# Attention gate's columns computed as seven products of halves, and attention groups merged where the last group is computed

## The chip, the cores and the metric

The kernel runs on one core of a Trainium2 chip. A core has five engines with a queue each: TensorE (PE in the profile; PEld is its weight load), VectorE (DVE), ScalarE (ACT), GpSimd (POOL) and SyncE (SP, which here only issues DMAs). An engine takes its instructions in the order in which they stand in its queue, and waits on semaphores of the others. The time is the device time of one execution in microseconds (us).

## The reference, cut to what matters

One decoder block on x of 2048 tokens x 1024 channels, in float32:

```python
h = rms_norm(x, norm_w) * (1 + scale) + shift
a, b, g_conv, q, k, v, g_attn, m_conv, m_attn = split(h @ w_in)   # 10240 columns
u = silu(layer_norm(conv31(a * sigmoid(b)))) * silu(g_conv);  y_conv = u @ w_conv_out
for g, (window, dilation) in enumerate(((128, 1), (512, 4), (2048, 16))):   # 4 heads of 128 each
    o[g], lse[g] = dilated_window_attention(q, k, v of the group's heads)
o = sum_g softmax_g(lse)[g] * o[g]            # the merge of the three groups, per token and head
y_attn = (o * silu(g_attn)) @ w_attn_out      # g_attn: 512 columns, the attention gate
x + gate * ((sigmoid(m_conv) * y_conv + sigmoid(m_attn) * y_attn) @ w_out)
```

## The kernel before, in words

Every float32 product is made of three TensorE products of halves of the mantissa (high x high, low x high, high x low), so each operand is kept as a `hi` and a `lo` tile. `h` lies transposed in SBUF in eight tiles for each of hi and lo: `(kh, t)` holds channels 512·kh on and tokens 512·t on.

The program has four stages that matter here.

1. **Units.** Twelve units, one for each group and head (`GROUPS = (1, 2, 0)`: the strided groups first, the dense one, group 0, last), each of 16 steps of 128 tokens. A step's `project_step` (L379) makes q, k, v of its tokens by `z_tokens` (L361, its matmul is L370): 24 matmuls of 128x384 into the bank `pz`, of which there are two. ScalarE then squares (L387), GpSimd takes the inverse root (L113, L114), VectorE normalises `qk` straight out of the bank (L398) and turns it (L405 to L408). After L398 the bank is free. The attention of a block of 128 queries is four parts (`attend_step`, L420): transposes `ptq`, scores `ps` with the row minimum and the exponential, transposes `ptp`, value product `po`. A `Flow` lays one part of each block in flight into the middle of a step's 24 matmuls; the order on TensorE is written by hand in this way, and the order on the other engines is set by a scheduler. Each block's output, with its row minimum and row sum (`osb`, 130 columns), goes to `acc_d` in DRAM for all three groups.
2. **Gate and merge.** 32 steps `(half, j)`, each of two heads and 128 tokens. `merge_z` (L497) is `z_tokens` with 256 of the gate's 512 columns into `pzg`. `merge_load` reads the three groups' outputs back from `acc_d`, `merge_weights` (L481) makes the groups' weights for two steps at a time, `merge_step` (L502) merges (L508, L510), takes the gate's silu by tanh (L513, L514), multiplies on GpSimd (L515) and transposes the product (`pta`, L520) into `ai_d`. The quarters S1 to S4, sums of quarters of `h` that were made earlier and lie in `s_d`, are split into hi and lo during the last of these steps, in place of tiles of `h` that are no longer needed.
3. **Conv and gates** (L885 on). Two halves of 1024 tokens, 20 jobs (`quad`, L940) in each: a job makes 2 x 128 columns for 1024 tokens as a 2x2 block product by seven products of 12 matmuls of 128x512 (with the sums S1 to S4 on the side of `h` and T1 to T4 on that of the weights), where eight would be needed directly. `column_steps` loads, combines and splits the weights. `ab_quad` makes the conv's input, `gate_quad` the other gates. The 31 taps of the conv run on VectorE, three or four operations per product (`run_conv`), beside the products.
4. **Projections** of the attention and conv branches, norm, output.

## Time and profile before

| | us |
|---|---|
| median of three runs | 2416.08 (2413.98 to 2416.86) |
| the profiled execution | 2415.89, its span 2414.0 |
| first gate matmul to first matmul of conv and gates | 1091.9 to 1205.1 |
| conv and gates | 1205.1 to 1966 |

TensorE is busy 98% of the span. In a timeline a row has start, duration, engine, line, operation and tiles, and in brackets the idle time before it with what ended it; matmuls overlap in their pipeline, so what one costs is the distance to the next start, not its duration. In windows the first number is the length, then come busy times with counts by engine and the granted TensorE clock (1.00 is full).

### The profile page before, as it was taken

How to read it: one execution, taken by the hardware profiler on the slowest of the kernel's cores; microseconds unless marked ns; L12 is line 12 of the kernel's file. 1: busy time of each engine (PE TensorE's matmuls, PEld its weight loads, DVE VectorE, ACT ScalarE, POOL GpSimd, SP SyncE). 2: the span in 40 equal slices, each digit the busy share in tenths (PEclk: the TensorE clock that was granted, in tenths of full speed). 3: DMA queues.
4: the chain of work that ended last, by engine and by line, in shares of the span. 5: the costliest groups of instructions: out<-in, count | busy, mean ns of one | idle time of the engine just before them, and what ended most of it. 6: DMA issues, size and time to landing. Idle time of an engine off the chain costs nothing.

```text
span 2414.0 us, 39453 instructions
## 1 busy us (share of the span) xinstructions
PE 2374.5 (98%) x12785; PEld 2119.2 (88%) x12785; DVE 1727.6 (72%) x3959; ACT 995.1 (41%) x2790; POOL 809.4 (34%) x931
## 2 busy tenths in 40 slices
PE   6999999999999999999999999999999999999999
PEld 2989999999999999999888888878888888878887
DVE  5855655555555565566879999989999977787654
ACT  5833433433444343444553444454444444332221
POOL 4421111111111111112357777775565530000221
PEclk8999999999999999999999999999999999999999
DMA  7633543544452222115654453674454469876553
GB/s 257 219 114 109 160 125 100 152 141 144 150 153 86 67 76 60 33 51 164 207 194 151 161 166 127 191 249 127 141 151 128 146 196 316 301 234 190 183 162 100
DMA packets 349467, 372.98 MB, mean 155 GB/s; under 512 B 29704, under 2 KB 251176, under 8 KB 349262
## 3 DMA queue, kind: packets, MB, share of 16 engines
q1 hardware_dynamic: 335966, 346.80, 46.3%
q10 hardware_dynamic: 13296, 23.66, 2.7%
q8 instruction: 102, 1.67, 0.3%
q14 instruction: 103, 0.84, 0.1%
HBM read 231.74 MB, written 138.61 MB: 153 GB/s over the span
## 4 chain that ended last, share of the span: by engine, by line
PE 90%; DMA 5%; DVE 2%; ACT 2%; POOL 1%; issue 1%; SPq 0%; ACTq 0%; DVEq 0%; POOLq 0%
PE pz L370 31%; PE paab L955 7%; PE yc L1231 6%; PE oa L1513 4%; PE ya L1231 4%; PE pag_g_d L955 4%; PE pag_mc_d L955 4%; PE pcab L955 3%; PE pag_ma_d L955 3%; PE pzg L370 3%; PE ps L442 3%; PE po L461 3%; PE oc L1513 2%; PE pcg_mc_d L955 2%; PE pcg_g_d L955 2%; PE ptq L432 2%
## 5 line engine op out<-in xcount | busy, mean ns | idle before, releaser
L370 PE MATMUL pz<-wh_u,hT_lo 128*128 128x384 f32 x1536 | 538.3, 351 | 5.8 <-DVE hT_lo L289 4.1
L370 PE MATMUL pz<-wh_u,hT_hi 128*128 128x384 f32 x1536 | 519.1, 338 | 4.6 <-ACT wh_u L346 2.6
L370 PE MATMUL pz<-wl_u,hT_hi 128*128 128x384 f32 x1536 | 520.1, 339 | 0.2
L398 DVE SCALAR_TENSOR_TENSOR qk<-pz,st,wqk 128x128 f32<-128x128 f32 x384 | 116.9, 346 | 319.9 <-POOL st L114 319.7
L113 POOL TENSOR_SCALAR st<-st 128x2 f32<-128x2 f32 x192 | 47.3, 246 | 814.5 <-ACT sq L387 814.5
L370 PEld LDWEIGHTS pz<-wh_u,hT_lo 128*128 128x128 f32 x1536 | 290.2, 189 | 9.0 <-DVE hT_lo L289 5.0
L370 PEld LDWEIGHTS pz<-wh_u,hT_hi 128*128 128x128 f32 x1536 | 291.4, 190 | 7.3 <-ACT wh_u L346 3.4
L370 PEld LDWEIGHTS pz<-wl_u,hT_hi 128*128 128x128 f32 x1536 | 290.5, 189 | 1.7 <-DVE wl_u L349 1.3
L434 ACT ACTIVATE qkT<-ptq 128x256 f32<-128x256 f32 x192 | 73.9, 385 | 419.9 <-PE ptq L432 419.4
L1033 DVE SCALAR_TENSOR_TENSOR ce<-us,pair_taps,ce 128x512 f32<-128x512 f32 x240 | 179.5, 748 | 1.7
L1004 DVE SCALAR_TENSOR_TENSOR ce<-ut,chan,ce 128x512 f32<-128x512 f32 x240 | 179.2, 747 | 0.0
L1017 DVE SCALAR_TENSOR_TENSOR cq<-ut,chan,cq 128x512 f32<-128x512 f32 x208 | 156.4, 752 | 4.2
L919 POOL TENSOR_TENSOR slT<-wT,shT 128x512 fp32r<-128x512 f32 x97 | 129.0, 1332 | 75.5 <-ACT shT L918 75.4
L387 ACT ACTIVATE sq<-pz 128x128 bf16<-128x128 f32 x384 | 106.2, 277 | 101.3 <-PE pz L370 94.4
L114 POOL TENSOR_TENSOR st<-st,mhalf 128x2 f32<-128x2 f32 x192 | 136.7, 712 | 16.0
L918 ACT ACTIVATE shB<-wB 128x512 fp32r<-128x512 f32 x120 | 75.5, 631 | 152.5 <-issue 44.5
L918 ACT ACTIVATE shT<-wT 128x512 fp32r<-128x512 f32 x100 | 63.1, 631 | 154.2 <-issue 65.7
L919 POOL TENSOR_TENSOR slB<-wB,shB 128x512 fp32r<-128x512 f32 x77 | 102.2, 1328 | 69.2 <-ACT shB L918 68.8
L447 ACT ACTIVATE sm<-sm,osb 128x128 f32<-128x128 f32 (+1 forms) x192 | 88.8, 462 | 62.1 <-DVE osb L445 59.1
L461 PE MATMUL po<-lv,pT 128*128 128x128 f32 x600 | 97.2, 273 | 0.0
L461 PEld LDWEIGHTS po<-lv,pT 128*128 128x128 f32 x600 | 93.0, 189 | 0.5 <-issue 0.5
L445 DVE CUSTOM_DVE_ANT_0 sm<-ps,mask 128x128 f32<-128x128 f32 (+1 forms) x192 | 68.2, 356 | 26.5 <-PE ps L442 26.4
(665 smaller groups left out, 6285.0 us busy)
## 6 DMA issues: line engine op xcount, KB each, us to landing
wB<-in_w_in_dram SPq DMA_DIRECT2D x140, 256.0 KB, 3.4
qkv_d<-qkv SPq DMA_DIRECT2D x128, 192.0 KB, 2.2
wT<-tT_d SPq DMA_DIRECT2D x80, 256.0 KB, 2.8
raw_u<-in_w_in_dram SPq DMA_DIRECT2D x93, 192.0 KB, 3.0
lqk<-qkv_d SPq DMA_DIRECT2D x128, 128.0 KB, 2.4
tT_d<-wB ACTq DMA_DIRECT2D x60, 256.0 KB, 2.8
acc_d<-osb SPq DMA_DIRECT2D x192, 65.0 KB, 1.7
at<-acc_d SPq DMA_DIRECT2D x64, 195.0 KB, 3.6
```

The source lines that it names most:

```text
L114: nc.gpsimd.tensor_tensor(dst, scratch[:, :n], mhalf[:, :n], op=ALU.pow)
L370: nc.tensor.matmul(pz[:, :width], part(a, k, P * j, P), w[:, :width], start=(m == 0), stop=(m == 23))
L398: nc.vector.scalar_tensor_tensor(qk[:, 2 * i : 2 * i + 2].rearrange("p a b -> p (a b)"), pz[:, P * i : P * i + P], st[:, 2 + i : 3 + i], w ...
L461: nc.tensor.matmul(po[:, :P], box["pT"][:, P * i : P * i + P], vt, start=(i == 0), stop=(i == nk - 1))
L918: nc.scalar.activation(h, q[name], AF.Copy)
L919: eng.tensor_tensor(l, q[name], h.bitcast(F32), op=ALU.subtract)
L955: nc.tensor.matmul(ps, w, x, start=(m == 0 and ps.name not in first), stop=(m == 11 and not more), skip_group_check=True)
L1004: stt(box["e"], e[:, 1 + j : 513 + j], chan[:, cb, 2 * j : 2 * j + 1], box["e"], op0=ALU.mult, op1=ALU.add)
L1017: stt(box["o"], o[:, 2 + j : 514 + j], w, psum_o, op0=ALU.mult, op1=ALU.add)
L1033: stt(dst, box["both"][:, 1 + j : 513 + j], pair_taps[:, cb, j : j + 1], box["e"], op0=ALU.mult, op1=ALU.subtract if j == 0 else ALU.add)
L1231: nc.tensor.matmul(pz, w, xx, start=(m == 0), stop=(m == len(terms) - 1))
L1513: nc.tensor.matmul(ps, y, w, start=(m == 0 and ps.name not in begun), stop=(m == 11 and not more), skip_group_check=True)
```

## The change

The gate's 512 columns leave stage 2, which is gone. They become four more jobs of stage 3, `ag_quad`, two in each half (jobs 15 and 17 of the first 22, and 38 and 39 of 44): seven products of 12 matmuls each. The job's `sink` takes silu of the product, loads the merged attention output `ai_d`, multiplies on GpSimd and writes `ag_d`, which the attention projection reads in place of `ai_d`.

The merge moves into the units of group 0 (the last four). Only groups 1 and 2 write to `acc_d`. A block of group 0 loads their 2 x 130 columns with its first part (`fetch`, issued on ScalarE's queue), and with its third part `weigh` makes the three weights for its 128 rows: a copy on GpSimd, five small operations on VectorE, one exponential and one scaled copy on ScalarE, and one 128x128 multiply-add on VectorE. `values` then multiplies and adds straight out of the bank `po`, where a copy stood. `turn_o`, a fifth part, transposes two blocks' outputs and stores them to `ai_d`.

The last unit goes through its blocks from 3 on, round to 2, so that the tiles of `h` come free in turn; S1, S2 and S3 are split in its steps 6 to 8 and 10 to 15, S4 among the first products. The attention of its last blocks, 7 turns, is laid between the first 13 products of stage 3, which begins with two gate jobs (one before). The strided blocks that run beside group 0 come every 2.5 steps (3.5 before), the sums for S1 to S4 in units 3 to 7 (4 to 10 before). The conv's operations are handed out at 2.9 and 3.1 per product.

```diff
+        def weigh():
+            st, part = box["st"], box["part"]
+            nc.gpsimd.tensor_copy(st[:, 0:2, 1:NG], part[:, :, P:].rearrange("p g k -> p k g"))
+            nc.vector.tensor_reduce(st[:, 4, 0:1], st[:, 0, :], op=ALU.min, axis=AX.X)
+            nc.scalar.activation(st[:, 2], st[:, 0], AF.Exp, scale=-1.0, bias=st[:, 4, 0:1])
+            nc.vector.tensor_mul(st[:, 3], st[:, 2], st[:, 1])
+            nc.vector.tensor_reduce(st[:, 4, 1:2], st[:, 3], op=ALU.add, axis=AX.X)
+            nc.vector.reciprocal(st[:, 4, 2:3], st[:, 4, 1:2])
+            nc.vector.scalar_tensor_tensor(st[:, 3], st[:, 2], 4.0, st[:, 4, 2:3].to_broadcast([P, NG]), op0=ALU.mult, op1=ALU.mult)
+            nc.scalar.activation(part[:, 0, :P], part[:, 0, :P], AF.Copy, scale=st[:, 3, 1:2])
+            nc.vector.scalar_tensor_tensor(part[:, 0, :P], part[:, 1, :P], st[:, 3, 2:3], part[:, 0, :P], op0=ALU.mult, op1=ALU.add)
...
+        def turn_o():
+            if j % 2 == 0:
+                return
+            pt = bank("t" if u == NG * NH - 1 and j in (13, 15, 1, 3) else "o", f"pta{n}")
+            for b, o in enumerate((state["even"], box["o"])):
+                nc.tensor.transpose(pt[:, P * b : P * b + P], o[:, :P], ident)
+            asb = mp.tile([P, 256], F32, tag="asb", name=f"asb{n}")
+            nc.scalar.activation(asb, pt[:, :256], AF.Copy)
+            nc.sync.dma_start(ai_d[h, :, P * j - P : P * j + P], asb)
...
+            if g == 0:
+                nc.vector.scalar_tensor_tensor(o[:, :P], po[:, :P], box["st"][:, 3, 0:1], box["part"][:, 0, :P], op0=ALU.mult, op1=ALU.add)
...
+        def fetch():
+            part = box["part"] = mp.tile([P, 2, ACC_W], F32, tag="part", name=f"part{n}", bufs=5)
+            nc.scalar.dma_start(part, acc_d[h][P * j : P * j + P])
...
-        pz = merge_z(0, j, cur, hooks)
...
-        turns += merge_step(half, j, pz, state)
...
+    def ag_quad(half, _, cb, got):
+        def sink(t, col, z, free=None):
+            th = z if free is None else free
+            sl = slice(1024 * half + 512 * t, 1024 * half + 512 * t + 512)
+            ait = gpa.tile([P, 512], F32, tag="ai", name=f"ag{half}_{cb}_{t}_{col}", bufs=2)
+            nc.sync.dma_start(ait, ai_d[cb + col, :, sl])
+            nc.scalar.activation(th, z, AF.Silu)
+            nc.gpsimd.tensor_mul(th, th, ait)
+            nc.sync.dma_start(ag_d[cb + col, :, sl], th)
...
+        todo[9 : 9] = [(ag_quad, half, None, cb) for cb in (0, 2)]
+        jobs += [todo.pop(0) for _ in range(2 - 2 * half)]
...
+        if at < TAIL and at % 2 == 0:
+            if own:
+                main.enter(own.pop(0))
+            for f in main.turn():
+                f()
```

VectorE, in the middle of a unit of group 0 (the last one, step 8, before; the third, step 8, after). `ps` are scores, `stm` the small tile of minima, sums and weights, `part` the other groups' outputs. Before:

```order
L445 ISA sm_5_13641,osb_5_13640<-ps_5_13637,mask 128x256
L445 ISA osb_5_13640 128x1
L349 TENSOR_TENSOR wl_ga_4_13654<-raw_ga_4_13651,wh_ga_4_13653 128x256
L462 COPY osb_14_13540<-po_14_13688 128x128
L398 SCALAR_TENSOR_TENSOR qk_8_13674<-pz_8_13608,st_8_13666,wqk 128x128 x2
L405 TENSOR_TENSOR t_8_13677<-qk_8_13674,tab_111 128x256
```

and after:

```order
L461 ISA sm_5_13071,stm_5_13070<-ps_5_13066,mask 128x256
L461 ISA stm_5_13070 128x1
L477 TENSOR_REDUCE stm_5_13070<-stm_5_13070 128x1
L350 TENSOR_TENSOR wl_u_4_13086<-raw_u_4_13083,wh_u_4_13085 128x384
L479 TENSOR_TENSOR stm_5_13070<-stm_5_13070 128x3
L480 TENSOR_REDUCE stm_5_13070<-stm_5_13070 128x1
L481 RECIPROCAL stm_5_13070<-stm_5_13070 128x1
L482 SCALAR_TENSOR_TENSOR stm_5_13070<-stm_5_13070 128x3
L461 ISA sm_14_13123,osb_14_13122<-ps_14_13120,mask 128x128
L461 ISA osb_14_13122 128x1
L484 SCALAR_TENSOR_TENSOR part_5_12983<-part_5_12983,stm_5_13070 128x128
L402 SCALAR_TENSOR_TENSOR qk_8_13106<-pz_8_13024,st_8_13098,wqk 128x128 x2
```

The whole of `weigh` now stands between a block's scores and the next normalisation out of `pz` (L398 before, L402 after).

TensorE, where stage 3 begins. Before, only transposes of the gated output stand among its first products; and ahead of it the gate matmuls, `pzg`, with a `pta` between them; a piece of them:

```order
L370 MATMUL pzg_3_15897<-wh_ga_0_14464,hT_hi_251 128x256
L370 MATMUL pzg_3_15897<-wl_ga_0_14465,hT_hi_251 128x256
L370 MATMUL pzg_3_15897<-wh_ga_0_14464,hT_lo_259 128x256
L520 MATMUL pta_1_15901<-ident,sg_1_15831 128x128 x2
L370 MATMUL pzg_3_15897<-wh_ga_1_14516,hT_hi_251 128x256
```

After, between the first product (`pag`) and the second (`pbg`) of stage 3:

```order
L897 MATMUL pag_g_d_0_15099<-hT_hi_252,first_w 128x512
L491 MATMUL pta_13_15124<-ident,osb_12_14725 128x128
L491 MATMUL pta_13_15124<-ident,osb_13_14812 128x128
L500 MATMUL po_14_15130<-lv_13_14568,pT_14_14974 128x128
L500 MATMUL po_14_15130<-lv_14_14659,pT_14_14974 128x128
L468 MATMUL ptp_15_15134<-ident,sm_15_14990 128x128 x2
L451 MATMUL ps_0_15148<-qkT_0_14998 128x128
L436 MATMUL ptq_1_15155<-ident,lqk_1_14931 128x128 x2
L897 MATMUL pbg_g_d_0_15100<-hT_hi_256,first_w 128x512
```

A whole turn of attention parts now lies there, and six more between the later ones.

ScalarE among the same products, before (one function table is loaded for the silu, and stays):

```order
L918 ACTIVATE shB_0_0_16025<-wB_0_0_15990 128x512
L918 ACTIVATE shB_0_0_16070<-wB_0_0_15992 128x512
L1081 ACT_TABLE_LOAD
L1081 ACTIVATE spare_hi<-spare_hi 128x512
L961 ACTIVATE spare_hi<-pag_g_d_0_16009 128x512
```

and after, in the seventh product:

```order
L860 ACTIVATE shB_0_2304_15347<-wB_0_2304_15086 128x512
L903 ACTIVATE spare_hi<-pag_g_d_0_15099 128x512
L493 ACTIVATE asb_15_15284<-pta_15_15281 128x256
L463 ACTIVATE sm_2_15309,stm_2_15308<-sm_2_15309,stm_2_15308 128x256
L1023 ACT_TABLE_LOAD
L1023 ACTIVATE spare_hi<-spare_hi 128x512
L463 ACT_TABLE_LOAD
L463 ACTIVATE sm_3_15319,stm_3_15316<-sm_3_15319,stm_3_15316 128x256
```

The silu of the gate job (L1023) and the exponential of the attention (L463) alternate here: five table loads stand where one stood, four more in all.

More of the change, by code (lines that the diff above doesn't have):

```diff
@@ L749, in tile_hybrid_block @@
                         extra.setdefault((14, 14, 23, 23)[i], []).append(lambda rest=rest: rest.pop(0)())
[L750 removed]
+                if u and 4 <= j < 4 + KC and not last_unit:
                     extra = spread_load(loads[j - 4])
[L752 removed]
+                for m, f in side.pop((u, p), ()):
                     extra.setdefault(m, []).append(f)
@@ L786, in tile_hybrid_block @@
-    turns = []
-    for j in range(3):
-        hooks = {}
-        for m in (4, 15):
-            if own and (j, m) != (0, 15):
-                main.enter(own.pop(0))
-            hooks[m] = main.turn()
-        pz = merge_z(0, j, cur, hooks)
-        if j < 2:
-            turns += merge_step(0, j, pz, state, "qkv", ("qk", "t3")[j])
-    assert not own and not main.parts and not beside.parts
-    wk_c.__exit__(None, None, None)
-    wk_c = tc.tile_pool(name="mg", bufs=2, reuse_waits="tile")
@@ L873, in tile_hybrid_block @@
-    close_side("at0")
+    own.append(held_part)
+    for args in landed:
+        quarter_split(*args, nc.vector)
+    assert not beside.parts and not placing
     spare_c.__exit__(None, None, None)
```

314 lines of the change are left out of this document (134 added, 180 removed).

## The prediction

> **What bounds the kernel now.** I read the page's first part, then windows by stage, the groups and waits of TensorE in the gate's stage, and timelines where a price was missing.
>
> ```profile
> span 2414.0 us, 39453 instructions
> PE 2374.5 (98%) x12785; PEld 2119.2 (88%) x12785; DVE 1727.6 (72%) x3959; ACT 995.1 (41%) x2790; POOL 809.4 (34%) x931
> ```
>
> TensorE bounds the whole: a change is worth what it takes from TensorE's row of instructions, less the waits it puts there. All sums below are made against the profiled execution (2415.89, of which 1.9 lies outside the span); it stands 0.2 below the median of 2416.08, so no correction is made. The stage that the change removes, and the one that it lengthens (length, then busy times PE, PEld, DVE, ACT, POOL, then the granted clock):
>
> ```profile
> 1091.86:1205.14 113.28, 106.67 (x873) 104.90 (x872) 86.28 (x296) 59.58 (x193) 33.17 (x41) 0.98 0.65 197
> 1205.14:1966.00 760.86, 758.30 (x3336) 626.77 (x3337) 702.74 (x1016) 345.45 (x606) 504.84 (x396) 1.00 0.51 161
> ```
>
> The gate and merge take 113.28 us. TensorE's groups in them (busy and mean count overlapping ends, so only the counts and the idle time are used):
>
> ```profile
> L370 PE MATMUL pzg<-wh_ga,hT_hi 128*128 128x256 f32 x256 | 75.7, 296 | 0.0
> L370 PE MATMUL pzg<-wl_ga,hT_hi 128*128 128x256 f32 x256 | 73.2, 286 | 0.0
> L370 PE MATMUL pzg<-wh_ga,hT_lo 128*128 128x256 f32 x256 | 72.8, 285 | 0.0
> L520 PE MATMUL pta<-ident,sg 128*128 128x128 f32 x60 | 12.0, 285 | 5.6 <-POOL sg L515 5.6
> L461 PE MATMUL po<-lv,pT 128*128 128x128 f32 x20 | 3.0, 273 | 0.0
> L453 PE MATMUL ptp<-ident,sm 128*128 128x128 f32 x8 | 1.5, 272 | 0.0
> L442 PE MATMUL ps<-qkT,qkT 128*128 128x128 f32 x6 | 1.2, 275 | 0.0
> L442 PE MATMUL ps<-qkT 128*128 128x128 f32 x6 | 1.2, 275 | 0.0
> L432 PE MATMUL ptq<-ident,lqk 128*128 128x128 f32 x4 | 0.8, 272 | 0.0
> ```
>
> These are 768 gate matmuls and 104 short ones. The prices are starts of matmuls far apart in TensorE's timeline, with nothing waiting between:
>
> ```profile
> 1088.80 0.61 PE L461 MATMUL po<-lv,pT 128*128 128x128 f32 x4
> 1090.05 0.42 PE L370 MATMUL pz<-wh_u,hT_lo 128*128 128x384 f32 x1
> ...
> 1175.81 0.28 PE L370 MATMUL pzg<-wl_ga,hT_hi 128*128 128x256 f32 x1
> 1178.45 0.28 PE L370 MATMUL pzg<-wh_ga,hT_lo 128*128 128x256 f32 x1
> ...
> 1799.67 0.39 PE L955 MATMUL pag_mc_d<-A_hi,shT 128*128 128x512 f32 x1
> 1825.73 0.39 PE L955 MATMUL pag_mc_d<-S_lo,shT 128*128 128x512 f32 x1
> ```
>
> Twelve short matmuls stand between the first two rows, 1.25/12 = 0.104 us each. 22 steps lie between the next two: 2.64/22 = 0.120 for a 128x256. 115 lie between the last two: 26.06/115 = 0.2266 for a 128x512.
>
> **The change, part by part.**
>
> *The gate's columns.* Removed: 768 matmuls at 0.120 = 92.2 us, and what stood around them. The short matmuls (transposes of the gated output, attention parts) come back elsewhere in the same number: 104 x 0.104 = 10.8 stays. So 113.28 - 10.8 = 102.5 us goes. Added: 4 jobs x 7 products x 12 = 336 matmuls of 128x512 at 0.2266 = 76.1. That is 102.5 - 76.1 = **26.4 us less**. Of it 92.2 - 76.1 = 16.1 is plain arithmetic (seven products for eight); 10.3 is lost time of the stage that goes, of which these rows show the larger part:
>
> ```profile
> PE pta L520 <- POOL sg L515: 5.6, 6, 2.9
> PE pag_g_d L955 <- ACT shB L918: 1.0, 1, 1.0
> PE paab L955 <- ACT spare_hi L1081: 2.4, 1, 2.4
> 1164.66 0.69 PE L520 MATMUL pta<-ident,sg 128*128 128x128 f32 x2 [2.86 <-POOL sg L515]
> 1164.70:1168.10 3.40, 3.40 (x16) 3.40 (x17) 3.40 (x10) 1.48 (x5) 2.46 (x3) 0.51 0.81 217
> ```
>
> 5.6 us of waits for the gated product and 1.0 at the first product of conv and gates; behind the 2.86 us wait the clock was granted at 0.51 for 3.4 us, which costs 3.4 x 0.49 = 1.7; the other 2.0 are restarts behind transposes. The third wait lies between the halves of conv and gates; it is not touched and stays.
>
> *The merge in group 0's units.* TensorE gets nothing for it; the other engines do, 64 times. What covers it, from a step of group 0 in VectorE's timeline, with ScalarE's first square of the next `pz` bank but one:
>
> ```profile
> 992.08 0.61 DVE L398 SCALAR_TENSOR_TENSOR qk<-pz,st,wqk 128x128 f32<-128x128 f32 x2 [0.60 <-POOL st L114]
> 994.68 0.08 DVE L445 DVE_READ_ACCUMULATOR2_ANT osb<- 128x1 f32 x1
> 997.80 0.61 DVE L398 SCALAR_TENSOR_TENSOR qk<-pz,st,wqk 128x128 f32<-128x128 f32 x2 [3.04 <-POOL st L114]
> 998.44 0.43 DVE L405 TENSOR_TENSOR t<-qk,tab 128x256 f32<-128x256 f32 x1
> 1001.64 0.28 ACT L387 ACTIVATE sq<-pz 128x128 bf16<-128x128 f32 x1 [0.53 <-PE pz L370]
> ```
>
> A step lasts 5.7 us (992.08 to 997.80); VectorE works 2.68 of it and is idle for 3.04 before it normalises. What `weigh` costs is seen in the old merge:
>
> ```profile
> 1130.35 0.21 ACT L488 ACTIVATE stm<-stm 128x12 f32<-128x12 f32 x1
> 1130.59 0.30 DVE L489 TENSOR_TENSOR stm<-stm,at 128x12 f32<-128x12 f32 x1 [0.34 <-ACT stm L488]
> 1131.34 0.17 DVE L492 SCALAR_TENSOR_TENSOR stm<-stm,mn 128x12 f32<-128x12 f32 x1
> 1131.59 0.70 ACT L508 ACTIVATE om<-at,stm 128x128 f32<-128x128 f32 x2 [1.03 <-DVE stm L492]
> 1132.03 0.65 DVE L510 SCALAR_TENSOR_TENSOR om<-at,stm,om 128x128 f32<-128x128 f32 x2 [0.18 <-ACT om L508]
> ```
>
> Five small VectorE operations at 0.17 to 0.30 make about 1.0, the multiply-add about 0.33 (0.65 for two): 1.3 more per step, 4.0 of 5.7. As a chain: the score's exponential about 0.7, the weights' own 0.21, the small ones 1.0, the scaled copy 0.4, the multiply-add 0.33, some 0.3 between: 2.9 us. It stands ahead of the next normalisation, which frees the bank of `pz`. It fits into the 3.04 us of idle time; and were it late, the normalisation ends at 998.41 and its bank is wanted again at about 1001.6, when TensorE has filled the other: 3.2 more. I take 0; the upper bound is rival C. What comes with it is covered too: the load of `part` is issued with a block's first part and used with its third, two steps or 11 us later; a small copy per block on GpSimd; one issue more on ScalarE; the copy of `turn_o` on ScalarE in place of that of `pta`. Value products no longer copy but multiply-add out of `po`: the same operation count.
>
> In the last unit the quarters' splits (two 128x512 operations each) come on top: VectorE's demand is about 5 of 5.7. I take 0.5, the bound is 1.
>
> *The start of conv and gates.* ScalarE and VectorE now carry the last blocks' attention there. VectorE's price of a 128x512 operation, and ScalarE's of a function table and of an issue:
>
> ```profile
> L919 DVE TENSOR_TENSOR slB<-wB,shB 128x512 fp32r<-128x512 f32 x43 | 31.1, 728 | 11.2 <-ACT shB L918 11.0
> 1212.47 0.33 ACTq L923 DMA_DIRECT2D tT_d<-wB  x1
> 1214.15 1.28 ACT L1081 ACT_TABLE_LOAD   x1
> 1215.44 0.63 ACT L1081 ACTIVATE spare_hi<-spare_hi 128x512 f32<-128x512 f32 x1
> ```
>
> Between the last two normalisations and the rotated `lqk` of the very last block, VectorE's queue has ten 128x512 operations (7.3 us at 0.728) and a dozen short ones (by the rows above 0.2 to 0.6 each; those that can't run early, about 3.1). Counted from the end of the last projection, with 1 us until it can begin, that block is ready at 11.4. TensorE comes to its transposes after three products (36 x 0.2266 = 8.2) and one and a half turns of parts (14 x 0.104 = 1.4), at 9.6: a stall of 1.8. It lies between 0 (the first five, which are weights' low parts, run before the projection ends: 3.6 less) and 5.5 (none does and ScalarE's splits come late too); I take 1.8. The four more table loads cost ScalarE 5.1 us within about 30 us; its chain to the last probabilities comes to 28.0 after the last projection and TensorE to 27.9: 0.3 with the hand-over. Seven turns break the stream of products: 7 x 0.1 = 0.7. The wait of 1.0 at the first product is in the sum above as gone; I put 0.2 back. Together with the last unit: 0.5 + 1.8 + 0.3 + 0.7 + 0.2 = **3.5 us**.
>
> The Trainium skill ("ScalarE: Activation LUTs", What ACT_TABLE_LOAD costs) has a load at 1283 ns and about 1380 ns of drain, 2.66 us per switch, and its rule is to batch by set. The trace agrees on the load and shows no drain: the operation before ended at 1214.14, the load began at 1214.15, the next began 0.01 behind it. By the page four switches would be 10.6 us of ScalarE and not 5.1.
>
> *The conv.* It has as many operations as before, beside 28 products more. VectorE was busy 702.74 of 760.86 us (92%); with 76 us more and about 10% more of the columns' work it has more room, so I cost it at 0. What is added is on GpSimd, four 128x512 multiplies per job:
>
> ```profile
> 1205.00:1586.00 381.00, 380.70 (x1679) 314.62 (x1680) 349.04 (x511) 173.75 (x308) 275.77 (x220) 1.00 0.53 170
> L979 POOL TENSOR_TENSOR spare_lo<-spare_lo 128x512 f32<-128x512 f32 x22 | 29.6, 1344 | 22.1 <-ACT spare_lo L961 22.1
> ```
>
> GpSimd is busy 276 of 381 us of the first half. A job lasts 19 us, and four multiplies at 1.344 add 5.4 to it: no cost while the job's other GpSimd work stays under 13.6, as its mean of 13.8 nearly does; the jobs beside it have the room.
>
> The sum: 2415.9 - 26.4 + 3.5 = **2393 us**.
>
> **The rivals.**
>
> *A: the start of conv and gates costs more.* For it: two engines come within 2 us of TensorE there by my counts, and table loads alternate. If each of the four switches holds TensorE for its whole 1.28 (5.1) in place of the 0.3, and one wait exceeds 2.5 us, so that half a clock follows as it did above (1.7): 2393 + 4.8 + 1.7 = about 2400. Against it: attention parts are a turn of two products, 5.4 us, apart. By the Trainium skill's drain it would be 4 x 1.38 = 5.5 more, 2405. The same notes ("TensorE: Matmul & The Clock Gate", Part 1) let the clock fall after an idle window of about 3.4 us; the trace has it fall after 2.86, so a shorter wait than theirs can do it.
>
> *B: GpSimd holds up the products of the gate jobs* (bank or weights come late behind its multiplies). The bound is all four jobs' multiplies on TensorE's path, 4 x 5.4 = 21.6: 2415, no gain. For it: 72% busy. Against it: TensorE waited 0.2 us there for all four gate kinds before. A third to a half of the bound gives 2400 to 2404.
>
> *C, the other side: `weigh` sets the pace of group 0's units.* Its chain goes VectorE, ScalarE, VectorE, ScalarE, VectorE, each in queue order behind other work. If the chain exceeds idle time and slack (3.04 + 3.2 = 6.2 against the 2.9 estimated), every step waits. Gain and loss are equal at 22.9/64 = 0.36 us per step; a pace of 6.3 in place of 5.7 gives 64 x 0.6 = 38: 2431. It needs the chain to be more than twice as long as its parts; what speaks for it is that five hand-overs can each find a 0.6 us operation ahead.
>
> **How the numbers follow.** The forecast, 2387 to 2398 by its own bounds (no stalls beyond 0.7 + 0.2 at 2390, some 3 lower if restarts and the wait between the halves vanish too; transition at its bound of 5.5 above), has 0.67; A 0.17; B 0.06; C 0.10, of which 0.08 ends slower and 0.02 level. 0.2% is 4.8 us, about what a measurement can tell from no change. Faster: 0.67 + 0.17 + 0.05 = 0.89; same 0.03 (C's 0.02, B's 0.01); slower 0.08. The range 2387 to 2407 takes in A and the middle of B; it leaves out C, B's end, and some 0.04 below.
>
> **What would show it.** Right: from the first unit to the first product of conv and gates TensorE keeps its pace; the steps of group 0 stay at 5.3 to 5.7 us, VectorE's idle time before its normalisation falls from 3.0 to under 2; the waits name no `sg`; conv and gates last 760.9 + 76.1 + the moved short matmuls of seven turns + about 3. Wrong: `pz` waits for `qk` in the last four units (C); waits over 2.5 us behind a table load, with the clock near 0.5 after them (A); products waiting for GpSimd's low parts in jobs 15, 17, 38 and 39 (B); conv operations left after the last product, so that VectorE ends the stage.

## The result, and the profile after

The changed kernel takes 2402.41 us (median of four runs, 2399.66 to 2403.95) against 2415.93 us; the ratio is 0.9944, with a 95% interval of 0.9927 to 0.9961. That is 13.5 us less. The forecast was 2393, so it has the direction and the range, but the gain is a little over half of the 23 us that it gave. The profiled execution took 2403.49 us, of which 2401.7 are its span. One execution further below, the profiled one of the kernel with the late split, ran at a clock of 0.85 from start to end and took 2600.26 us, so no time or wait is read from it.

The first part of the page, then windows by stage: the third unit of group 0 before and after, and the first half of conv and gates after (length, then busy times PE, PEld, DVE, ACT, POOL, the granted clock, DMA share and GB/s). Before:

```profile
910.13:1001.36 91.23, 91.23 (x604) 90.97 (x604) 50.43 (x185) 37.06 (x149) 14.83 (x32) 1.00 0.19 53
```

After, the page and the windows:

```profile
span 2401.7 us, 38846 instructions
PE 2357.0 (98%) x12353; PEld 2089.6 (87%) x12353; DVE 1738.0 (72%) x4091; ACT 1021.6 (43%) x2850; POOL 844.0 (35%) x1003
```

```profile
915.12:1008.81 93.69, 93.69 (x627) 93.18 (x627) 70.64 (x286) 47.27 (x191) 17.24 (x48) 1.00 0.23 63
...
1098.71:1538.21 439.50, 428.24 (x1906) 353.90 (x1905) 384.30 (x595) 206.62 (x380) 309.14 (x251) 0.99 0.53 171
```

TensorE has 432 matmuls less, 768 less 336, as counted. In the unit, VectorE works 20.2 us more, 1.26 per step (the prediction had 1.3), and TensorE doesn't wait for it; the unit is 2.46 us longer for 23 more short matmuls. In the first half of conv and gates TensorE is idle for 11.3 of 439.5 us. TensorE's waits after, those that are new or grown:

```profile
PE paab L897 <- ACT spare_hi L1023: 5.9, 1, 5.9
PE ptq L436 <- DVE pT L470: 3.5, 5, 2.0
PE ptq L436 <- DVE lqk L412: 2.2, 1, 2.2
PE pz L371 <- DVE qk L402: 1.6, 3, 0.9
PE pcg_g_d L897 <- DVE osb L502: 0.9, 1, 0.9
```

The first row is the wait at the change of halves, 2.4 us before. The second (its longest, 2.0) and the third lie at the start of conv and gates, between attention parts. The fourth is small, but it is the sign that the prediction named for rival C: 1.1 of its 1.6 us fall in the last unit of group 0, where nothing waited for `qk` before. These are the places of the first three in TensorE's timeline, and then windows with the clock behind the later two:

```profile
1104.76 0.44 PE L436 MATMUL ptq<-ident,lqk 128*128 128x128 f32 x2 [2.01 <-DVE pT L470]
...
1113.85 0.63 PE L436 MATMUL ptq<-ident,lqk 128*128 128x128 f32 x2 [2.17 <-DVE lqk L412]
...
1538.21 0.79 PE L897 MATMUL paab<-A_hi,shB 128*128 128x512 f32 x1 [5.88 <-ACT spare_hi L1023]
```

```profile
1114.10:1117.10 3.00, 3.00 (x9) 2.41 (x8) 3.00 (x12) 2.38 (x5) 0.00 (x0) 0.50 0.79 237
1538.20:1543.20 5.00, 4.99 (x12) 3.93 (x13) 4.11 (x6) 3.17 (x6) 2.82 (x3) 0.50 1.02 326
```

Where the gain went, stage by stage, counted from starts of matmuls in the two traces (us against the sum of matmuls alone, which is 2414.0 - 26.4 = 2387.6; a short matmul that moved counts 0.104, a 128x512 of the new jobs 0.2266):

| place | predicted | found |
|---|---|---|
| program's start, to group 0's first unit | 0 | -0.4 |
| group 0's units, beyond their 51 more short matmuls (56 transposes come in, 5 others leave) | 0.5 | 1.9 |
| start of conv and gates: waits, clock, restarts | 3.0 | 7.8 |
| change of halves: wait, clock behind it | 0 | 4.6 |
| together | 3.5 | 13.9 |

Of the 1.9 us in the units, 1.1 are the waits for `qk` in the last one. So the arithmetic of the change holds, and the two places behind the units gave 9.4 us more of it back than the prediction allowed.

What stood on VectorE at the first of these two, and beside it on GpSimd, from the timeline (VectorE's subtractions on 128x512 take about 0.68 alone):

```profile
1103.42 0.69 DVE L861 TENSOR_TENSOR slT<-wB,shT 128x512 fp32r<-128x512 f32 x1
1104.02 0.34 DVE L502 SCALAR_TENSOR_TENSOR osb<-po,stm,part 128x128 f32<-128x128 f32 x1
1104.28 0.41 DVE L470 COPY pT<-ptp 128x256 f32<-128x256 f32 x1
...
1107.41 1.78 DVE L861 TENSOR_TENSOR slB<-wB,shB 128x512 fp32r<-128x512 f32 x1
1109.11 1.77 DVE L726 TENSOR_TENSOR S_lo<-s,S_hi 128x512 fp32r<-128x512 f32 x1
1110.81 1.48 DVE L409 TENSOR_TENSOR t<-qk,tab 128x256 f32<-128x256 f32 x1
1112.22 0.41 DVE L410 TENSOR_TENSOR lqk<-qk,tab 128x256 f32<-128x256 f32 x1
...
1107.35 1.29 POOL L852 TENSOR_TENSOR wT<-wB,wB 128x512 f32<-128x512 f32 x1
1108.61 1.73 POOL L852 TENSOR_TENSOR wB<-wB,wB 128x512 f32<-128x512 f32 x1
1110.29 1.72 POOL L852 TENSOR_TENSOR wB<-wB,wT 128x512 f32<-128x512 f32 x1
```

The copy `pT`, for which the first `ptq` waits, stands behind five low parts (L861), the last of which is shown. Before the second `ptq`, three of VectorE's operations take 1.48 to 1.78 us, exactly while GpSimd combines the second job's weights (L852); the same `t` and `lqk` differ by 1.07 us. The trace before had this price too. In its conv and gates, the 0.728 that the prediction took is the mean of one group of low parts; two other groups of the same shape stand in the same list at 1.05 and 1.15 us. Of the nine `slT` there, six have no GpSimd operation beside them and take 0.68, three have one and take 1.78:

```profile
L919 DVE TENSOR_TENSOR slT<-wB,shT 128x512 fp32r<-128x512 f32 x9 | 9.3, 1050 | 2.8 <-ACT shT L918 2.8
L840 DVE TENSOR_TENSOR A_lo<-landingA,A_hi 128x512 fp32r<-128x512 f32 x9 | 10.3, 1150 | 0.3 <-ACT A_hi L839 0.3
```

### The profile page after: what moved, and what is told of

The parts are those of the page before. It is cut to its first block, busy times and chain, and to the rows that moved or that the text cites. A ratio compares the mean times of both kernels' runs of the same rounds, so it can differ in the third digit from the quotient of the medians.

```text
span 2401.7 us, 38846 instructions
## 1 busy us (share of the span) xinstructions
PE 2357.0 (98%) x12353; PEld 2089.6 (87%) x12353; DVE 1738.0 (72%) x4091; ACT 1021.6 (43%) x2850; POOL 844.0 (35%) x1003
## 4 chain that ended last, share of the span: by engine, by line
PE 88%; DVE 3%; DMA 2%; ACT 2%; POOL 1%; issue 1%; ACTq 0%; POOLq 0%; DVEq 0%
PE pz L371 30%; PE paab L897 7%; PE yc L1204 6%; PE oa L1486 4%; PE pcab L897 4%; PE pag_mc_d L897 4%; PE ya L1204 3%; PE pag_g_d L897 3%; PE pag_ma_d L897 3%; PE po L500 3%; PE ps L451 3%; PE pcg_g_d L897 2%; PE oc L1486 2%; PE pbab L897 2%; PE paag L897 2%; PE pcg_mc_d L897 2%
## 5 line engine op out<-in xcount | busy, mean ns | idle before, releaser
L402 DVE SCALAR_TENSOR_TENSOR qk<-pz,st,wqk 128x128 f32<-128x128 f32 x384 | 117.0, 346 | 270.5 <-POOL st L115 269.3
L861 POOL TENSOR_TENSOR slT<-wT,shT 128x512 fp32r<-128x512 f32 x107 | 143.3, 1339 | 80.6 <-ACT shT L860 78.4
L860 ACT ACTIVATE shB<-wB 128x512 fp32r<-128x512 f32 x130 | 82.1, 632 | 172.3 <-issue 65.5
L860 ACT ACTIVATE shT<-wT 128x512 fp32r<-128x512 f32 x110 | 69.4, 631 | 165.8 <-issue 73.0
L861 POOL TENSOR_TENSOR slB<-wB,shB 128x512 fp32r<-128x512 f32 x85 | 110.3, 1298 | 77.0 <-ACT shB L860 76.5
L409 DVE TENSOR_TENSOR t<-qk,tab 128x256 f32<-128x256 f32 x192 | 82.5, 430 | 5.5
L861 POOL TENSOR_TENSOR slT<-wB,shT 128x512 fp32r<-128x512 f32 x57 | 75.4, 1330 | 27.1 <-ACT shT L860 27.0
```

Source lines behind the costliest of these rows:

```text
L402: nc.vector.scalar_tensor_tensor(qk[:, 2 * i : 2 * i + 2].rearrange("p a b -> p (a b)"), pz[:, P * i : P * i + P], st[:, 2 + i : 3 + i], w ...
L860: nc.scalar.activation(h, q[name], AF.Copy)
L861: eng.tensor_tensor(l, q[name], h.bitcast(F32), op=ALU.subtract)
```

## The experiments

Times are medians beside runs of the kernel before on the same chip. Single runs of one kernel differ by up to 9 us (the kernel before, on one chip: 2411.36 to 2420.11), part of it in the program's start and in its last stage, which no edit touches, and the median of the kernel before is 2415.86 to 2418.86 by chip. So kernels are compared by their ratios, and by these only the three combinations below (start and conv jobs together, both edits of the start with the pins, more landing tiles) lie clear of the changed kernel's 0.9927 to 0.9961. What a single edit did is read from waits and stage lengths, one trace each. "The first half without the gap at its end" is counted from the first product's start to the start of the last matmul ahead of the gap.

**The weights left out, and made three times.** Is the merge in group 0's units hidden, and by how much?

```diff
         def weigh():
-            st, part = box["st"], box["part"]
...
+            nc.gpsimd.memset(box["st"][:, 3], 1.0)
```

> Edit: left out is the making of the merge's weights and the scaling of the other groups' outputs (five small operations, an exponential, a scaled copy and a multiply-add per block); a memset on GpSimd puts 1 for the weights, the loads and the multiply-add out of po stay. Theory (merge hidden in group 0's units): units 8 to 10 last 93.7 to 94.4 us with it and the same without it, within 0.3; of the 2.5 us that they are longer than before the change, all but a few tenths are the moved transposes (14 to 16 a unit at 0.104). The start of conv and gates gains about 1 us. Rival (weigh paces the units): they fall by 1 us or more each.

```diff
         def weigh():
...
             nc.gpsimd.tensor_copy(st[:, 0:2, 1:NG], part[:, :, P:].rearrange("p g k -> p k g"))
+            nc.vector.tensor_reduce(st[:, 4, 0:1], st[:, 0, :], op=ALU.min, axis=AX.X)
+            nc.scalar.activation(st[:, 2], st[:, 0], AF.Exp, scale=-1.0, bias=st[:, 4, 0:1])
+            nc.vector.tensor_mul(st[:, 3], st[:, 2], st[:, 1])
+            nc.vector.tensor_reduce(st[:, 4, 1:2], st[:, 3], op=ALU.add, axis=AX.X)
+            nc.vector.reciprocal(st[:, 4, 2:3], st[:, 4, 1:2])
...
```

> Edit: minimum, exponential, product, sum and reciprocal of the weights are made three times over; the result is the same. This adds two rounds of 1.4 us to the chain and 8 operations of 0.155, 1.25 us, to VectorE's 4.41 of 5.86 us per step. Theory (the merge has slack until chain or VectorE's work exceeds the step): the chain is 2.9 + 2.8 = 5.7 against 6.2 of room, VectorE at 5.66 of 5.86 per step: units 8 to 10 grow by less than 1 us each (94 to 95), the last unit, with the quarters' splits, by 2 to 5. Rival C of the prediction with a lower threshold (every step already waits): each unit grows by 16 x 1.4 = 22 us or, by VectorE's work alone, by over 5.

The third unit without the weights:

```profile
915.67:1009.36 93.69, 93.69 (x627) 93.18 (x627) 52.94 (x190) 39.74 (x159) 15.75 (x48) 1.00 0.23 63
```

and with three rounds of them:

```profile
917.06:1010.75 93.69, 93.69 (x627) 93.18 (x626) 76.70 (x415) 53.84 (x224) 17.30 (x48) 1.00 0.23 62
```

Both last 93.69 us, as in the changed kernel, and the two units ahead of it are within 0.15. So inside these units `weigh` costs TensorE nothing, left out or with three rounds; the last unit too lasts 88.4 with three rounds (88.4 to 90.4 over all kernels), where 2 to 5 us more were expected. The eight more operations a step cost VectorE 0.38 us and not 1.25: the trace has such short ones 0.07 to 0.2 us apart, each 0.15 long. Rival C is refuted by the first of the two: with the weights and without them all four units are equally long within 0.15 us. The second doesn't test its threshold, since the scheduler didn't keep the longer chain ahead of the normalisation: in this unit one chain goes from 963.1 to 970.4 us, with a normalisation (L402 at 966.11) between its rounds. In the changed kernel the chain of a block goes from 961.1 to 963.9, 2.8 us as estimated (2.9), and the normalisation follows at 964.23. At the start of conv and gates `weigh` isn't quite free: the first half without the gap at its end is 432.1 us without it, 433.2 in the changed kernel and 434.3 with three rounds, where a `ptq` waits 2.2 us for the weights themselves (`stm`). Times: 2401.25 without, 2404.4 with three rounds, one run each, too few to tell them apart.

**Tanh gates first.** Do the alternating tables hold TensorE (rival A)?

```diff
-        gates = [(GC0, g_d, AF.Silu), (MC0, mc_d, AF.Tanh), (MA0, ma_d, AF.Tanh)]
+        gates = [(MC0, mc_d, AF.Tanh), (GC0, g_d, AF.Silu), (MA0, ma_d, AF.Tanh)]
```

> Edit: the first four gate jobs are those of the tanh gate mc, and the silu gate's follow (the other way round in the changed kernel); the exponential and the tanh share a table, so one table load stands there and not five. Theory (loads hidden): TensorE's waits at the start stay at 2.0 and 2.2 us, 2402 +-1. Rival (the alternation of tables holds TensorE, rival A of the prediction): 4 x 1.28 us of ScalarE come off its path, the start is 3 to 5 us shorter, 2398.

2400.86 us, ratio 0.9937 (0.9922 to 0.9952). No table load stands in the start of conv and gates any more, and its two waits are the same:

```profile
PE ptq L436 <- DVE pT L470: 3.5, 5, 2.0
PE ptq L436 <- DVE lqk L412: 2.2, 1, 2.2
```

The first half without the gap at its end is 432.9 us against 433.2. The wait for `osb` (0.9) went. So the four loads cost TensorE at most about 1 us, and rival A's mechanism is wrong.

**The second job's combinations on VectorE.** Do operations on GpSimd hold VectorE's?

```diff
-            (nc.vector if first else nc.gpsimd).tensor_tensor(dst, x0, x1, op=ALU.subtract)
+            (nc.vector if on_dve else nc.gpsimd).tensor_tensor(dst, x0, x1, op=ALU.subtract)
...
-        return column_steps(half, c0, c1, on_vector, i == 0)
+        return column_steps(half, c0, c1, on_vector, i == 0, i < 2)
```

> Edit: the four combinations of weights of the second job (T1 to T4) are made on VectorE and not on GpSimd. Theory (a shared port): VectorE's operations on two SBUF tensors take 1.5 to 1.8 us beside GpSimd's (1106 to 1112 us) in place of 0.42 to 0.68; without GpSimd they fall back to these, VectorE gains 3.8 us and pays 3 x 0.6 = 1.9 for the combinations ahead of the last block; the second wait of the start falls from 2.2 to 0.5 or less and the clock behind it stays above 0.9: 2 to 3.5 us less, 2399 to 2400. Rival (VectorE has too much there, whoever runs beside it): the wait grows by 1.9 to about 4 and the time to 2404.

2398.66 us, ratio 0.9932 (0.9915 to 0.9948). The same operations on VectorE, the combinations L852 now among them, and the clock after them:

```profile
1105.53 0.68 DVE L861 TENSOR_TENSOR slB<-wB,shB 128x512 fp32r<-128x512 f32 x1
1106.12 0.68 DVE L726 TENSOR_TENSOR S_lo<-s,S_hi 128x512 fp32r<-128x512 f32 x1
1106.72 0.41 DVE L409 TENSOR_TENSOR t<-qk,tab 128x256 f32<-128x256 f32 x1
...
1108.00 0.68 DVE L852 TENSOR_TENSOR wB<-wB,wB 128x512 f32<-128x512 f32 x1
```

```profile
1108.00:1114.00 6.00, 5.84 (x32) 4.91 (x31) 5.76 (x18) 5.79 (x9) 0.00 (x0) 1.00 0.77 259
```

The slow operations are back at 0.68 and 0.41, the second wait falls from 2.2 to 0.2 us, the clock stays at 1.00, and the first half is 3.6 us shorter (435.9 against 439.5; without the gap 429.8 against 433.2). About half of that is the wait, the other half the clock. That VectorE and GpSimd held each other there is shown: VectorE does more work and is done sooner. The Trainium skill ("SBUF — State Buffer", Who interferes with whom) has the rule: a VectorE instruction with two SBUF inputs contends with a GpSimd instruction that reads SBUF, and one blocks until the other is finished. The runs agree; the price here was 1.07 to 1.1 us per operation.

**The first job's weights split late.** Is it the order on VectorE that makes the first wait?

```diff
-            eng.tensor_tensor(l, q[name], h.bitcast(F32), op=ALU.subtract)
+            i2 = eng.tensor_tensor(l, q[name], h.bitcast(F32), op=ALU.subtract)
+            if pin and len(made) > 1:
+                tc.keep_in_program_order(i2)
...
-    for at in range(7):
-        prepare(at)
...
+    prepare_to(1)
...
         next(running[i], None)
-        prepare(at + 7)
-        if s4:
-            quarter_split(*s4.pop(0), nc.vector)
         if at < TAIL and at % 2 == 0:
...
                 f()
+        prepare_to(at + min(7, 2 + max(0, at - 3)))
+        if s4:
+            quarter_split(*s4.pop(0), nc.vector)
```

> Edit: the first job's weights from its third product on are split two products ahead and not seven at once, the attention turn is written ahead of them, and their low parts are pinned behind it on VectorE; so one low part and one of S4's stands ahead of the copy pT that the turn waits for, where five stood, and none but one between it and the rotation of the last block, where five did. Theory (order on VectorE): the first wait of the start falls from 2.0 to 0.8 or less, the second from 2.2 to 1 or less, and with no wait over 2 us the clock stays full: 4 to 6 us less, 2397 to 2398. Rival (amount of VectorE's work): the products wait for their low parts instead, and the sum of waits in the first 40 us stays at 5 us, 2402.

2398.93 us (median of three, 2398.82 to 2403.52), ratio 0.9934 (0.9918 to 0.9951), which tells neither expectation from the other. The waits can't be read here; they are read below, in the kernel with the start and the conv jobs together, which has this edit.

**The rates of the conv at the change of halves.** The change hands out 1.5 operations in four jobs where the kernel before had 1, 1, 2, 2. Is that why the wait there grew?

```diff
-        due += 2.9 if i < half_jobs - 2 else 1.5 if i < half_jobs + 2 else 3.1
+        due += 2.9 if i < half_jobs - 2 else 1.0 if i < half_jobs else 2.0 if i < half_jobs + 2 else 3.1
```

> Edit: in the four jobs at the change of halves the conv's operations are handed out at 1.0, 1.0, 2.0, 2.0 per product, as before the change, and not at 1.5 in all four; the sum is the same. Theory (VectorE's queue): the 0.5 more conv operations per product in the last two jobs of the first half delay VectorE's splits of the quarters, these free their landing tiles late, and ScalarE waits in its queue for the next landing ahead of the copy out of PSUM; the wait of TensorE at the change of halves falls from 5.9 us to 2.4 (+-0.6), the lower clock behind it costs about 1 less: about 4.5 us less than the changed kernel, 2398. Rival (transfers): the gate jobs' added loads and stores fill the DMA engines there (busy share 0.93 to 1.05), so the wait stays at 5 to 6 and the time at 2402.

2403.15 us, ratio 0.9945 (0.9931 to 0.996); the wait is 5.2 us. But the edit didn't test its theory: the scheduler fills VectorE's queue by what is ready, and in the order of its instructions hardly a row moved, and none but a semaphore wait between 1070 and 1950 us. So this is in effect a second trace of the changed kernel, and it shows how far two traces of one order differ: 5.2 against 5.9 us at the change of halves. At the start the wait for `lqk` fell from 2.2 to 0.6 us, but only since the clock fell one product earlier, behind the first wait (0.64 over the 4.3 us after it), and TensorE came later: without the gap at its end the first half is 432.5 us, against 433.2.

**Three gate jobs behind the last conv job.** This does move VectorE's queue.

```diff
-            for _ in range(((1, 1, 2, 1, 2, 1, 2, 2), (1, 2, 1, 2, 2, 1, 2, 3))[half][cb]):
+            for _ in range(((1, 1, 1, 1, 2, 1, 2, 3), (1, 2, 1, 2, 2, 1, 2, 3))[half][cb]):
```

> Edit: in the first half three gate jobs stand behind the last conv job, as before the change, and not two (gate jobs per conv job 1, 1, 1, 1, 2, 1, 2, 3 in place of 1, 1, 2, 1, 2, 1, 2, 2). Unlike the rates, this moves VectorE's queue: ahead of the change of halves fewer of the last job's taps stand between the splits of the quarters. Theory (VectorE's queue at the change of halves): the wait there falls from 5.2 to 6.5 us in the kernels run so far to 2.4 (+-0.8): about 3.5 to 4.5 us less than the changed kernel, 2398. Rival (transfers of the gate jobs fill the DMA engines): the wait stays over 5, 2402.

2400.41 us, ratio 0.9927 (0.9909 to 0.9945); the wait stays at 5.1 us. VectorE has 12 taps in the 24 us ahead of the first product of the second half, where the changed kernel has 15 and the kernel before 14; so fewer taps alone don't shorten it. A product in the first half waits 1.0 us anew (`paab` for `spare_hi`).

**Start and conv jobs together:** the combinations on VectorE, the late split and the three gate jobs.

> Edit: the second job's combinations on VectorE, the first job's weights split late and pinned behind the attention turn, and three gate jobs behind the last conv job, together. Theory (two disturbed places, start and change of halves, each by what stands in VectorE's queue): the waits at the start fall from 4.2 to under 1.5 us, that at the change of halves to 2.4, the clock falls only behind the latter: 4 to 5 + 4 = 8 to 9 us less than the changed kernel, 2393 to 2394. Rival (the waits move on to the products and the next parts): 2398 or more.

2395.95 us, ratio 0.9906 (0.9891 to 0.992). Its waits:

```profile
PE paab L900 <- ACT spare_hi L1026: 5.2, 1, 5.2
PE ptq L436 <- DVE pT L470: 2.0, 5, 0.5
PE po L500 <- DVE pT L470: 0.7, 1, 0.7
```

At the start no wait is over 0.7 us: the first one was the five low parts ahead of `pT`. The first half without the gap at its end is 429.1 us, 4.1 less than in the changed kernel and 0.7 less than with the combinations alone. That is not all that the order gives: the three gate jobs bring a wait of 1.1 us into this half (`paab`, 1.0 in the kernel with this edit alone). Counted by waits between attention parts and first products, the combinations alone leave 3.6 us, both edits 1.5. So GpSimd's share of the start's gain is the larger, with the clock, and the order's about 2 us. At the change of halves nothing is gained.

**The splits pinned on ScalarE.** In the changed kernel ScalarE's timeline ahead of the change of halves reads:

```profile
1533.07 0.61 ACT L860 ACTIVATE shT<-wT 128x512 fp32r<-128x512 f32 x1
1535.22 0.63 ACT L725 ACTIVATE S_hi<-landingS 128x512 fp32r<-128x512 f32 x1 [1.54 <-DMA landingS<-s_d]
1536.53 0.63 ACT L725 ACTIVATE S_hi<-landingS 128x512 fp32r<-128x512 f32 x1 [0.67 <-DMA landingS<-s_d]
1537.06 0.61 ACT L860 ACTIVATE shT<-wT 128x512 fp32r<-128x512 f32 x1
1537.58 0.58 ACT L1023 ACTIVATE spare_hi<-pag_ma_d 128x512 f32<-128x512 f32 x1
```

The last row frees the bank for which TensorE has waited since 1532; it stands behind two splits of quarters that wait for their transfers.

```diff
+        if half == 1 or name == "S4":
+            tc.keep_in_program_order(i1)
         if half == 0 and name == "S4":
-            tc.keep_in_program_order(i1)
             tc.keep_in_program_order(i2)
```

> Edit: the high parts of the second half's quarters are pinned on ScalarE where they are written; so 10 of the splits of sums stand there ahead of the tanh that frees the bank for the first product of the second half, where the changed kernel has 13, the kernel with three gate jobs behind the last conv job 14, and the kernel before 12. Theory (order on ScalarE: the tanh stands behind splits that wait for their landing): the wait at the change of halves falls from 5.9 us (5.1 to 6.5 in all kernels run) to 1 or less and the clock stays full behind it: 6 to 7.5 us less than the changed kernel, 2395 to 2396. Rival (the landings themselves are too slow: transfers, one landing tile for every fourth piece): the first products of the second half wait for their quarters instead, the waits in the 45 us behind the change of halves come to 4 us or more, the time to 2401 or more.

2400.53 us, ratio 0.993 (0.9915 to 0.9944). The wait is cut in two, 2.8 at the first product and 2.0 at the second:

```profile
PE paab L898 <- ACT spare_hi L1024: 2.8, 1, 2.8
PE pag_g_d L898 <- ACT spare_hi L1024: 2.0, 1, 2.0
```

The sum, 4.8, is what the rival had (4 or more), though not its time of 2401 or more. The first half is 2.6 us shorter, the second 1.2 longer.

**The same pins in the kernel before.**

> Edit: the same pins in the kernel before the change. Theory (order on ScalarE): its wait at the change of halves falls from 2.4 us to 0.5 or less, and the lower clock behind it (1.7 us) goes too: about 3.5 to 4 us less, 2412. Rival (landings too slow): no gain, 2416.

2420.6 us, ratio 1.0019 (1.0009 to 1.0028): slower by 0.2%, with waits of 4.0 and 0.6 us where 2.4 was. The order on ScalarE alone is not the cause.

**Both edits of the start, with the pins.**

> Edit: the second job's combinations on VectorE, the first job's weights split late and pinned behind the attention turn, and the pins of the second half's splits on ScalarE, together. Theory (both places are a matter of order in one queue): waits at the start under 1.5 us, at the change of halves 1 or less, clock full from the last unit to the end of the second half: 10 to 12 us less than the changed kernel, 2390 to 2392, which is the prediction's sum with its 3.5 us of waits. Rival (the waits move elsewhere): 2396 or more, as with both earlier edits without the pins.

2396.26 us, ratio 0.9911 (0.9896 to 0.9926), with 2.7 and 1.0 us at the change of halves. That is no better than with the three gate jobs in the place of the pins, within what these runs tell, and misses the 2390 to 2392 of the theory, though the clock did stay full from the last unit to the end of the second half.

**More landing tiles.** The quarters of the second half pass through four tiles; that of every fourth piece comes free only when GpSimd has made the low part.

```diff
+            i1 = nc.scalar.activation(h, q[name], AF.Copy)
+            if pin_hi:
+                tc.keep_in_program_order(i1)
...
-            own, tag = (gpa, "gt") if k < 3 else (cv, "ld")
-            raw = own.tile([P, 512], F32, tag=tag, name=f"landing{name}_{k}", bufs=3 if k < 3 else 1)
+            own, tag = gpa, "gt" if k < 3 else "ai"
+            raw = own.tile([P, 512], F32, tag=tag, name=f"landing{name}_{k}", bufs=4 if k < 3 else 2)
```

> Edit: beside the three edits of the kernel with all, the second half's quarters land in six tiles in place of four (every fourth piece in the two tiles of the gate jobs' loads, which are idle there, in place of one of its own, and four for the others in place of three), and the first two jobs' high parts of the second half are pinned too, so that ten splits of sums stand ahead of the tanh. Theory (the landings: each piece waits until VectorE or GpSimd has freed one of four tiles, then 3.5 to 5 us for its transfer; with the tanh behind such waits): the waits at the change of halves fall from 3.7 us (2.7 and 1.0) to 1 or less, with a full clock 3 to 4 us less than the kernel with all, 2392 to 2393. Rival (the DMA engines are full there, share 0.92 to 1.05, and what lands is late however many tiles there are): 3 us or more of waits stay, 2396.

2394.18 us, ratio 0.9897 (0.9881 to 0.9914): the lowest of all and clear of both kernels, but not of the two combinations before it. One wait is left at the change of halves:

```profile
PE paab L903 <- ACT spare_hi L1029: 2.1, 1, 2.1
```

No split waits ahead of it. Its chain, which in the changed kernel has a landing of 3.48 us just ahead of the tanh, goes through VectorE, where the addition for the last product (`spare_hi`, L930) stands behind taps and splits:

```profile
1520.77 1.05 DVE S_lo L726
...
1525.51 0.60 DVE spare_hi L930
...
1526.67 0.59 ACT spare_hi L1029
```

So the landings were part of the wait, with the tanh queued behind them, and when both are eased VectorE is next; which of the two, tiles or pins, took the landings out of the chain is not shown, since they were changed together. Neither end of the expectation was met: 1 or less, or 3 and more. Why the same chain gave 2.4 us in the kernel before and 5.9 in the changed one stays open: the changed kernel has 13 splits of sums ahead of that tanh, and before 12, but with 14 (three gate jobs behind) the wait is 5.1 and with 10 (pins) it is not gone. Full DMA engines don't explain it: in three windows of 10 us ahead of the wait their busy share is 0.66 to 0.75 in the changed kernel and 0.73 to 0.96 before. One rival is untested. The hold between VectorE and GpSimd is at work here too: `S_lo` takes 1.63 and 1.71 us in the chain of the changed kernel, and the low parts on VectorE in the last 45 us take 5.5 us more than 0.68 each, and 6.3 in the kernel before. So it may be a part of either wait, but these sums don't explain their difference.

## Why the prediction was right or wrong

- **The sum of matmuls: right.** 432 fewer, 768 at 0.120 against 336 at 0.2266, and the short ones come back: 56 transposes in the units, the rest among the first products. The waits for `sg` and the low clock of the old merge are gone. One label is loose: seven eighths of 92.2 us are 80.7, so "seven products for eight" is 11.5 of the 16.1; the other 4.6 come from the longer matmul, 0.2266 for 512 columns against twice 0.120.
- **The merge at nothing: right.** Its part on VectorE was sized at 1.3 per step and measured 1.26, its chain at 2.9 and measured 2.8. Whether the "3.2 more" of slack is there wasn't tested. The last unit, taken at 0.5, shows 1.1 us of waits for `qk` in this trace and none to 0.8 in the other kernels with the same weights.
- **The table loads: right that they are hidden,** with 0.3 for the exponential's chain. Rival A's 2400 lies near the measured time by luck: it names the place of about half of the loss by a wrong cause, and nothing of the other half. The Trainium skill's drain of 1380 ns ("ScalarE: Activation LUTs", What ACT_TABLE_LOAD costs) would have made it dearer; the activation behind a load that nothing else delayed starts 0.01 us after the load's end here as before the change, and taking the loads away didn't shorten the waits.
- **The start of conv and gates, 3.0 in all: too small, 7.8.** The step counted one arrival, that of the very last block; there were two, and `pT` behind five low parts was the other (2.0 us, taken at nothing). The clock fell behind the second (1.6 us, taken at nothing), and a product waits 0.9 for `osb`. The one stall that it has, 1.8, measured 2.2, but by luck: the rotated `lqk` was ready 15.0 us after the last projection (at the first product's start) and not 11.4, and TensorE came at 13.0 and not 9.6, since it had waited 2.0 before and had more short matmuls to do. The count of ten 128x512 operations is exact; their price, a mean of 0.728 us, isn't. Between 1107 and 1112 us three operations of this path had a GpSimd operation on SBUF beside them and cost 3.3 us more in all. With GpSimd out of the way and the order changed, what remains of the two waits is under 1 us.
- **"It is not touched and stays": wrong.** The wait at the change of halves went from 2.4 to 5.9 us, with 1.1 more for the clock. The change moves conv jobs, rates and one instruction on ScalarE there, which the diff shows and the working passed over. What stands in the wait's chain is shown (landings of the quarters, ScalarE's order, VectorE); which part of the change made it grow is not.
- **Rival B: not seen.** No product waits for GpSimd in the gate jobs of the attention. **Rival C: refuted**, since the four units are as long with `weigh` as without.

## What to carry to other kernels

Work that moves from a stage of its own under other work is cheap where the cover is long and even (64 steps here, 1.9 us lost), and dear where stages meet: there the order of each queue, and what runs beside it, set the time, so list what stands ahead of each instruction that TensorE waits for on all engines, also at seams that the change seems not to touch. A mean duration of VectorE's operations on two SBUF tensors (0.728 here) is no price where GpSimd works in the same microseconds (1.77); look for its work there before using it.

## What was not expected of the hardware

- VectorE's operations on two SBUF tensors beside GpSimd's: 1.77 and 1.78 us in place of 0.68 (128x512), 1.48 in place of 0.41 (128x256). Which of the two begins first matters: in the kernel before, a low part that began 0.11 us behind a GpSimd operation took 1.76 us (at 1473.78), one that a GpSimd multiply met 0.53 us after its start kept 0.69 (at 1239.81). Taps of the conv, which read one operand from PSUM, kept 0.75 us beside GpSimd (at most 0.76 in 704).
- The clock fell behind some waits of about 2 us and not behind others: in the changed kernel to 0.50 for 3.4 us behind the second of two (2.0 and 2.2 us, 7 us apart); with the conv's rates behind the first, of 2.1; not behind the one of 2.0 with the combinations on VectorE, nor behind one of 2.7 with both edits of the start and the pins. What tells them apart in the traces is a grid. Stretches of lower clock begin and end on steps of 3.41 us. In thirteen traces, from 1090 to 2385 us, all 22 falls follow a step in which TensorE was busy for 1.49 us or less, and none follows one of the 4867 full-clock steps with 1.57 or more. The kernel with the pins alone has both cases. Its wait of 2.8 us is shared by two steps (2.05 and 1.95 us busy) and costs no clock; its wait of 2.0 lies in one (1.39 us busy) and halves the clock of the next:

```profile
1527.78:1531.19 3.41, 2.05 (x10) 1.35 (x8) 3.41 (x7) 2.79 (x6) 2.93 (x4) 1.00 0.73 222
1531.19:1534.61 3.42, 1.95 (x8) 1.61 (x9) 3.32 (x7) 2.05 (x4) 1.67 (x2) 1.00 0.88 247
1534.61:1538.02 3.41, 1.39 (x6) 0.85 (x5) 2.17 (x4) 2.15 (x4) 1.21 (x1) 1.00 1.11 313
1538.02:1541.43 3.41, 3.41 (x9) 2.64 (x9) 1.65 (x3) 1.63 (x3) 2.00 (x3) 0.50 1.08 361
```

So a wait of 2 to 3 us costs 1.7 us more or nothing by where it falls, which no one chooses, and a prediction can only give it a chance. The Trainium skill ("TensorE: Matmul & The Clock Gate", Part 1) names an idle window of about 3.4 us that runs free of the program. These rows agree on its length and that it runs free; that the array must be idle for all of it they contradict.

- Repeated tiny operations of VectorE are cheaper than their parts: eight more per step cost 0.38 us of its busy time, not eight times 0.155.
